# Third-chunk buffers, form loads by ScalarE's queue, sums joined one by one, and a projection moved, in a decoder layer's FFN and embedding stages

## The chip, the cores and the metric

One core of a Trainium2 chip runs the whole kernel in one launch. The metric is the device time in microseconds (us). The kernel before takes 2613.33 us, the median of three runs (2607.94 to 2615.98).

## What is computed

One decoder layer on 512 tokens with 2048 features, all in float32. A mixing part (linear recurrences and RWKV heads) comes first and is not touched here. Then:

```python
u = rmsnorm(h, ln_ffn)                                   # FFN
gate = causal_dwconv(u @ w_gate, conv_f_w, conv_f_b)     # 3 taps; w_gate, w_up: 2048 x 6144
h = h + (gelu(gate) * (u @ w_up)) @ w_down               # w_down: 6144 x 2048

u = rmsnorm(h, ln_ple)                                   # per-layer embedding
e = sigmoid(u @ w_ple_gate) * (p @ w_ple_proj)           # 2048 x 2048 and 256 x 2048
h = h + rmsnorm(e, ln_ple_post)
out = rmsnorm(h, ln_final)
```

## The kernel before

The engines are TensorE (PE; PEld is its weight loads), VectorE (DVE), ScalarE (ACT), GpSimd (POOL) and SyncE (SP). SP issues most transfers, POOL those that add to what is in memory on chip already (L1148, L1178).

**Splits.** Each float32 operand of a matmul is split in two parts of lower precision, `hi` and `lo`, and a product is three matmuls: hi x hi, hi x lo, lo x hi. A weight tile of 512 KB comes by DMA (`wraw`, or a buffer named `x` or `s` where it is combined first), ScalarE makes `whi` (L138) and VectorE `wlo` (L139). `whi` and `wlo` have three buffers each, `wraw` two. Lines 151, 152 and 155 split activations in the same way.

**Products of a block.** A block matrix product is made of seven products of sums of blocks instead of eight. The sums of activations are "forms". The sums of weights come from VectorE (L1131 in the gate stage, L1168 and L1174 in the down stage) and from POOL's adding transfers.

**The gate stage** (about 905 to 1886 us) has 48 units `n`, 24 for each of gate and up side by side. Unit `n` computes seven products, p1, p4, p2, q5, p7, p6, p3, each of 24 matmuls (L1280 to L1282). The order is fixed by hand: behind unit 0's products come the parts of unit 1, 2 and so on, so unit 1's p4 and p6 follow unit 0's p6 closely. p6 and p7 go to the two PSUM banks of the pool `wk`, the others to the six of `mm`. L1306 to L1312 combine the products; L1306 is the first reader of p6. After each even unit `conv` makes the convolution and the GELU (L1325 to L1331), which first multiplies by the tokens' scale of the RMS norm. That scale is spread over the partitions by `rstd_bcast`: four transposing matmuls (L210) into a `wk` bank and a copy by ScalarE (L212). It is called within unit 0, after p6. `spill` writes each finished chunk of the hidden layer to memory as forms (`rd`, `dd`).

**The down stage** (about 1886 to 2334 us) goes through groups of chunks, (0,3), (3,6), (6,9), (9,11), in 14 steps each: two output halves `b` times seven products in the order 1, 0, 4, 2, 3, 5, 6. A step multiplies each of the group's chunks, 12 matmuls a chunk (L1402 to L1404). `load_forms(g, j)` loads the form of product j of group g, three chunks of 256 KB each (L1355); `split_form` splits it two steps later. For the first group the first three forms are loaded during the last unit of the gate stage. Where they sit in SP's queue is up to the scheduler, while the order of VectorE and ScalarE is that of the code (`manual_schedule`, L1438). `down_unit` loads the weights. For product 1 of chunk c it loads two tiles and adds them (L1168); the buffers are given by numbers of `slot`: below 16 they are `x` buffers, from 16 to 43 `s` buffers (number less 16), 44 is the pool `e`. The third chunk's numbers 37, 38 and 39 are s21, s22 and s23, which hold forms of product p2 during the gate stage. After each step the result is copied by ScalarE in the first group (L1430) and added by VectorE in the others (L1428). At the end of each half of the last group seven sums join the seven products (L1435).

**After it** (2334 to 2394) the last chunk and the residual follow for each column block cb = 0, 2, 1, 3: `residual` (loads L1452, transposes L1456, L1458), `down_last` (its end on VectorE is L1468) and `to_features` (transposes L1477, splits L155). **The embedding stage** (2394 to the end) takes each column block's projection, 24 matmuls, and then its gate.

## Time and profile before

| | |
|---|---|
| median of three runs | 2613.33 us (2607.94 to 2615.98) |
| profiled execution | 2613.31 us |
| its span, first to last instruction | 2611.5 us |
| mean TensorE clock granted | 0.988 |
| busy: PE, DVE, ACT, POOL | 2543.5, 1904.5, 1249.5, 228.2 us |
| longest idle times of PE in the stages of the diff | 5.15 us at L210, 3.92 and 3.51 us at L1402, 1.96 us at L1477 and at L1402 |

A row of the waits names the instruction that waited, its releaser, the total in us, how often, and the longest. A row of a timeline has the start, the duration, the engine, line and operation, and in brackets the idle time before it and what ended it. A row of the windows has the busy time of each engine in a stretch with the clock granted to TensorE (1.00 is full speed). What lies between two matmuls' starts, not a matmul's own duration, is its cost in a dense run.

### The profile page before, as it was taken

Reading aid. Unit: us, or ns where it says so; the run is one execution under the profiler, and the core shown is the slowest. Engines: PE = TensorE matmul, PEld = TensorE weight load, DVE = VectorE, ACT = ScalarE, POOL = GpSimd, SP = SyncE. Lnnn points to the kernel's source line nnn. Section 1 sums busy time; section 2 is a strip of 40 time slices with the busy share of each in tenths; the row PEclk is TensorE's granted clock in tenths of the full one; section 3 lists DMA queues with packets and bytes.
Section 4 is the critical chain, followed back from the end, with each engine's and each line's share of the span. In section 5 each row is a group of like instructions: output and inputs, shape, how many; then the busy total and the mean of one; then the engine's idle time right before and its main releaser. Section 6 shows DMA issues by size and latency. Waiting matters only on the chain.

```text
span 2611.5 us, 51670 instructions
## 1 busy us (share of the span) xinstructions
PE 2543.5 (97%) x21922; PEld 2243.9 (86%) x21922; DVE 1904.5 (73%) x2603; ACT 1249.5 (48%) x1735; POOL 228.2 (9%) x251
## 2 busy tenths in 40 slices
PE   9989999999999989999999999999999999999997
PEld 8867777777777889999999999999978877777887
DVE  5764775667575978878788878887777786886447
ACT  6563555547433634444444444444466453434335
POOL 0010100101121010000000000000000000000001
PEclk9999999999999999999999999999999999999999
DMA  7222222222342666776677767777768777743333
GB/s 253 93 70 66 86 78 67 82 82 78 95 141 91 210 166 180 192 184 167 191 188 186 184 170 189 191 178 192 223 171 252 197 218 189 216 109 110 97 95 108
DMA packets 131304, 393.76 MB, mean 151 GB/s; under 512 B 14464, under 2 KB 26624, under 8 KB 131072
## 3 DMA queue, kind: packets, MB, share of 16 engines
q1 hardware_dynamic: 111200, 318.10, 35.9%
q0 software_dynamic: 19872, 72.36, 16.8%
q8 instruction: 171, 2.80, 0.4%
q14 instruction: 61, 0.50, 0.1%
HBM read 353.97 MB, written 36.44 MB: 149 GB/s over the span
## 4 chain that ended last, share of the span: by engine, by line
PE 62%; DVE 5%; DMA 2%; ACT 2%; issue 1%; POOL 0%; ACTq 0%; POOLq 0%; DVEq 0%
PE mm L1282 9%; PE mm L1281 9%; PE mm L1280 9%; PE mm L1403 5%; PE mm L1404 5%; PE mm L1402 5%; PE wk L1281 3%; PE wk L1282 3%; PE wk L1280 3%; PE mm L1519 2%; PE mm L1521 2%; PE mm L1520 2%; PE mm L168 2%; PE mm L170 2%; PE mm L172 1%; DMA wraw<-wd 1%
## 5 line engine op out<-in xcount | busy, mean ns | idle before, releaser
L138 ACT ACTIVATE whi<-x 128x1024 fp32r<-128x1024 f32 x296 | 313.5, 1060 | 441.5 <-PE mm L1281 232.6
L139 DVE TENSOR_TENSOR wlo<-x,whi 128x1024 fp32r<-128x1024 f32 x296 | 361.7, 1223 | 122.6 <-ACT whi L138 116.3
L138 ACT ACTIVATE whi<-wraw 128x1024 fp32r<-128x1024 f32 (+1 forms) x229 | 233.1, 1018 | 382.6 <-PE mm L170 186.4
L1282 PE MATMUL mm<-s,wlo 128*128 128x256 f32 x1432 | 406.3, 284 | 0.7 <-DVE wlo L139 0.7
L1280 PE MATMUL mm<-s,whi 128*128 128x256 f32 x1432 | 406.1, 284 | 0.9 <-ACT s L151 0.9
L139 DVE TENSOR_TENSOR wlo<-wraw,whi 128x1024 fp32r<-128x1024 f32 (+1 forms) x229 | 278.2, 1215 | 176.5 <-ACT whi L138 174.9
L1281 PE MATMUL mm<-s,whi 128*128 128x256 f32 x1432 | 406.1, 284 | 0.2 <-DVE s L152 0.2
L168 PE MATMUL mm<-x,whi 128*128 128x512 f32 x832 | 332.9, 400 | 1.2 <-DVE hT L458 0.9
L172 PE MATMUL mm<-x,wlo 128*128 128x512 f32 x832 | 332.8, 400 | 0.0
L170 PE MATMUL mm<-x,whi 128*128 128x512 f32 x832 | 331.6, 399 | 0.0
L1402 PE MATMUL mm<-whi,s 128*128 128x512 f32 x680 | 268.8, 396 | 10.7 <-ACT whi L138 10.6
L1280 PEld LDWEIGHTS mm<-s,whi 128*128 128x128 f32 x1432 | 275.8, 193 | 1.2 <-ACT s L151 1.1
L1282 PEld LDWEIGHTS mm<-s,wlo 128*128 128x128 f32 x1432 | 275.9, 193 | 0.9 <-DVE wlo L139 0.9
L1281 PEld LDWEIGHTS mm<-s,whi 128*128 128x128 f32 x1432 | 275.7, 193 | 0.4 <-DVE s L152 0.4
L1403 PE MATMUL mm<-wlo,s 128*128 128x512 f32 x680 | 269.9, 397 | 4.0 <-DVE wlo L139 4.0
L1404 PE MATMUL mm<-whi,s 128*128 128x512 f32 x680 | 268.6, 395 | 0.0
L168 PEld LDWEIGHTS mm<-x,whi 128*128 128x128 f32 x832 | 157.5, 189 | 37.2 <-issue 3.0
L172 PEld LDWEIGHTS mm<-x,wlo 128*128 128x128 f32 x832 | 157.5, 189 | 34.0 <-issue 1.9
L170 PEld LDWEIGHTS mm<-x,whi 128*128 128x128 f32 x832 | 157.4, 189 | 33.6 <-issue 1.8
L1148 POOL DMA_DIRECT2D x<-wgu x94 | 82.8, 880 | 955.2 <-DVE wlo L139 654.9
L1280 PE MATMUL wk<-s,whi 128*128 128x256 f32 x584 | 165.3, 283 | 0.0
L1281 PE MATMUL wk<-s,whi 128*128 128x256 f32 x584 | 165.3, 283 | 0.0
(570 smaller groups left out, 5510.6 us busy)
## 6 DMA issues: line engine op xcount, KB each, us to landing
x<-wgu SPq DMA_DIRECT2D x144, 512.0 KB, 4.1
x<-wgu POOLq DMA_DIRECT2D x94, 512.0 KB, 5.5
wraw<-wz SPq DMA_DIRECT2D x80, 512.0 KB, 3.5
wraw<-wgu SPq DMA_DIRECT2D x51, 512.0 KB, 4.1
x<-wd SPq DMA_DIRECT2D x34, 512.0 KB, 5.3
x<-wd POOLq DMA_DIRECT2D x32, 512.0 KB, 5.6
wraw<-wpg SPq DMA_DIRECT2D x31, 512.0 KB, 3.5
wraw<-wd SPq DMA_DIRECT2D x30, 512.0 KB, 4.0
```

What stands on the lines that cost most here:

```text
L138: nc.scalar.activation(hi, raw, AF.Copy)
L139: nc.vector.tensor_tensor(lo, raw, hi.bitcast(F32), ALU.subtract)
L168: nc.tensor.matmul(ps, hi[:, k, :], xh, start=first and i == 0, stop=False)
L170: nc.tensor.matmul(ps, hi[:, k, :], xl, start=False, stop=False)
L172: nc.tensor.matmul(ps, lo[:, k, :], xh, start=False, stop=last and i == n - 1)
L1148: nc.gpsimd.dma_start(g["s"], src(0, 0 if u == "p6" else 1), accum_op=ALU.add)
L1280: TE.matmul(ps, wh[:, k, :], xh, start=k == 0, stop=False)
L1281: TE.matmul(ps, wh[:, k, :], xl, start=False, stop=False)
L1282: TE.matmul(ps, wl[:, k, :], xh, start=False, stop=k == 7)
L1402: TE.matmul(ps, x[0][:, k, ts_], w[0][:, k, :], start=first and k == 0, stop=False)
L1403: TE.matmul(ps, x[0][:, k, ts_], w[1][:, k, :], start=False, stop=False)
L1404: TE.matmul(ps, x[1][:, k, ts_], w[0][:, k, :], start=False, stop=last and k == 1)
```

## The change

Six edits, all behind the mixing part.

1. The third chunk's buffers in the down stage (`down_unit`): s21, s22 and s23 become x13, x14 and x8. The result tiles `PT` that had x8, x13 and x14 move to s23, s21 and s22 in return.
2. `rstd_bcast` and the convolution of unit 0 move from the end of (0, p6) and (0, p3) to the end of (1, p6).
3. `load_form` issues on ScalarE's queue. Only the three forms loaded in the gate stage stay on SP's.
4. The seven sums of the last group's first half are made one after each step of its second half. Those of the second half are placed in the loop over cb: four ahead of `down_last(0)`, three ahead of `down_last(2)`.
5. The projection becomes a function. The one of column block 0 runs between `down_last(3)` and `to_features(3)`, with the loads and splits of the embeddings (`pT`) ahead of it.
6. Buffers of the features (`US`), of the residual and of the gains are numbered through `slot` and partly exchanged.

```diff
         def plain(kh, nh):
             self.pn += 1
-            return load(self.slot((2, 6, 39, 44, 44)[(self.pn - 1) % 5]), kh, nh)
+            return load(self.slot((2, 6, 8, 44, 44)[(self.pn - 1) % 5]), kh, nh)
         if i == 1:
-            self.d0[c], self.d1[c], self.dq[c] = plain(0, 0), load(self.slot((1, 5, 38)[c]), 0, 1), self.slot((0, 3, 37)[c])
+            self.d0[c], self.d1[c], self.dq[c] = plain(0, 0), load(self.slot((1, 5, 14)[c]), 0, 1), self.slot((0, 3, 13)[c])
...
-            if n == 0 and u == "p6":
-                self.rstd_bcast(acc, D, RMS_EPS, k2, rs, rt)
             if n == NF - 1:
                 if u in ("q5", "p1", "p4"):
-                    load_forms(0, ("q5", "p1", "p4").index(u))
+                    load_forms(0, ("q5", "p1", "p4").index(u), nc.sync)
...
-        def load_form(src, tag):
+        def load_form(src, tag, q=nc.scalar):
             t = T("s%d" % tag, 1, (128, 2, 2, 256), F32R)
-            nc.sync.dma_start(t[:, 1].bitcast(F32), src)
+            q.dma_start(t[:, 1].bitcast(F32), src)
...
             unit(n, u)
+            if n == 1 and u == "p6":
+                self.rstd_bcast(acc, D, RMS_EPS, k2, rs, rt)
+                c = B(9)
+                conv(0, o, c)
             if u != "p3":
                 continue
             p, o = n // 2, G_.pop(n)["out"]
+            if n == 0:
+                continue
...
-        PT = {i: [self.slot(n) for n in t] for i, t in enumerate(((43, 40), (8, 41), (15, 42), (4, 13), (12, 11), (7, 14), (10, 9)))}
+        PT = {i: [self.slot(n) for n in t] for i, t in enumerate(((43, 40), (39, 41), (15, 42), (4, 37), (12, 11), (7, 38), (10, 9)))}
...
+                if g + 1 == len(GROUPS) and b == 1:
+                    join(0, j)
...
-            if g + 1 == len(GROUPS):
-                for o, x, y, op in ((2, 2, 0, ALU.add), (5, 5, 0, ALU.add), (6, 6, 4, ALU.add), (6, 6, 2, ALU.add),
-                                    (1, 1, 2, ALU.subtract), (3, 3, 1, ALU.add), (4, 1, 4, ALU.subtract)):
-                    V.tensor_tensor(PT[o][b], PT[x][b], PT[y][b], op)
+        JOIN = ((2, 2, 0, ALU.add), (5, 5, 0, ALU.add), (6, 6, 4, ALU.add), (6, 6, 2, ALU.add),
+                (1, 1, 2, ALU.subtract), (3, 3, 1, ALU.add), (4, 1, 4, ALU.subtract))
+
+        def join(b, j):
+            o, x, y, op = JOIN[j]
+            V.tensor_tensor(PT[o][b], PT[x][b], PT[y][b], op)
...
         for cb in (0, 2, 1, 3):
             residual(cb)
+            if cb % 2 == 0:
+                for j in range(4 if cb == 0 else 3):
+                    join(1, j + 2 * cb)
             down_last(cb)
+            if cb == 3:
+                for k in range(2):
+                    r = T("e", 2, (128, 2, S))[:, 0]
+                    nc.sync.dma_start(r, A["pT"][k])
+                    t_ = self.slot(2 + k, F32R)
+                    self.split(t_[:, 0], t_[:, 1], r)
+                    px.append((t_[:, 0], t_[:, 1]))
+                pp = project()
             to_features(cb)
...
         for cb in range(4):
+            if cb:
+                pp = project()
```

The first place is TensorE in units 0 and 1 of the gate stage: `mm_11083` before and `mm_11077` after is the bank of (1, p4), `wk_11169` that of (1, p6), `wk_11221` that of (1, p7). Before:

```order
4018 L1282 MATMUL mm_10906<-s_1470_10136,wlo_11017 128x256
4019 L1280 MATMUL mm_11083<-s_1451_10117,whi_11045 128x256
4020 L1281 MATMUL mm_11083<-s_1451_10117,whi_11045 128x256
4021 L210 MATMUL wk_11077<-con,rsr_11012 128x128 x4
4022 L1282 MATMUL mm_11083<-s_1451_10117,wlo_11046 128x256
4023 L1280 MATMUL mm_11083<-s_1451_10117,whi_11045 128x256
```

In the new order the same four matmuls of L210 come after all 24 of (1, p6):

```order
4042 L1282 MATMUL mm_11077<-s_1454_10120,wlo_11046 128x256
4043 L1280 MATMUL wk_11169<-s_1455_10121,whi_11079 128x256
...
4066 L1282 MATMUL wk_11169<-s_1458_10124,wlo_11080 128x256
4067 L210 MATMUL wk_11206<-con,rsr_11012 128x128 x4
4068 L1280 MATMUL wk_11221<-s_1459_10125,x_1608_11110 128x256
```

L210 has moved past the rest of (1, p4) and past (1, p6), and the first to ask for the `wk` bank that L1306 frees is now (1, p6).

The second place is SP around the start of the down stage: `s22` and `s23` (before), `x8` (after) take the third chunk's weights, `s0` to `s20` forms, `e` and `x2` later weights. Before:

```order
511 L1355 DMA s12_2921_22050<-dd0_1_10814 128x512
512 L1355 DMA s13_2922_22052<-dd1_1_10816 128x512
513 L1355 DMA s14_2923_22054<-dd2_1_10818 128x512
514 L1355 DMA s15_2932_22116<-rd0_1_10790 128x2x256
515 L1355 DMA s16_2933_22118<-rd1_1_10792 128x2x256
516 L1160 DMA s22_2881_21866<-wd 128x1024
517 L1160 DMA s23_2880_21864<-wd 128x1024
518 L1355 DMA s17_2934_22120<-rd2_1_10794 128x2x256
519 L1160 DMA e_2913_21987<-wd 128x1024
```

And after (L1353 is the same load, L1335 the store to `rd`):

```order
506 L1160 DMA e_2905_21956<-wd 128x1024
507 L125 DMA wraw_2949_22190<-wd 128x1024
508 L1353 DMA s8_2864_21752<-dd2_1_10818 128x512
509 L1160 DMA x8_2880_21864<-wd 128x1024
510 L1160 DMA e_2913_21987<-wd 128x1024
511 L1335 DMA rd11_1_10812<-x11_2843_21606 128x1024
512 L1160 DMA x2_2916_22008<-wd 128x1024
```

The load into x8 follows the ninth form directly, the other of the pair (into x14) stands 22 rows before it, and the forms s9 to s20 are gone from SP. On ScalarE, in the first group, they stand behind the copies of a step; a name in brackets is a semaphore, DMAHW one of the eight that loads use in turn:

```order
1195 L1430 ACTIVATE s_2885_21902<-mm_21985 128x512
1196 L1430 ACTIVATE s_2885_21902<-mm_21986 128x512
1197 L1353 DMA s_2921_22050<-dd_1_10814 128x512 [waits DMAHW7_49]
1198 L1353 DMA s_2922_22052<-dd_1_10816 128x512 [waits DMAHW1_49]
1199 L1353 DMA s_2923_22054<-dd_1_10818 128x512 [waits DMAHW2_49]
1200 L138 ACTIVATE whi_22059<-x_2871_21797 128x1024 [waits DMASW6_49,PE_49,Activation_49]
```

Each of the three waits until an earlier load that used the same semaphore has landed, and the split L138 stands behind them.

The third place is VectorE at the turn from the first to the second half of the last group. L1435 (before) and L1444 (after) are the joins, L1428 and L1432 the sums of a step. Before:

```order
2262 L1428 TENSOR_TENSOR x_2897_21914<-x_2897_21914,mm_24873 128x512
2263 L1435 TENSOR_TENSOR x_2889_21906<-x_2889_21906,s_2885_21902 128x1024
2264 L1435 TENSOR_TENSOR x_2895_21912<-x_2895_21912,s_2885_21902 128x1024
2265 L1435 TENSOR_TENSOR x_2897_21914<-x_2897_21914,x_2893_21910 128x1024
2266 L1435 TENSOR_TENSOR x_2897_21914<-x_2897_21914,x_2889_21906 128x1024
2267 L1435 TENSOR_TENSOR x_2887_21904<-x_2887_21904,x_2889_21906 128x1024
2268 L1458 SCALAR_TENSOR_TENSOR x_2895_21912<-x_2895_21912,rsr_11012,wk_25202 128x512
2269 L1435 TENSOR_TENSOR x_2891_21908<-x_2891_21908,x_2887_21904 128x1024
2270 L1435 TENSOR_TENSOR x_2893_21910<-x_2887_21904,x_2893_21910 128x1024
2271 L1174 TENSOR_TENSOR x_3431_24826<-x_3431_24826,s_3448_24917 128x1024
```

After:

```order
2269 L1432 TENSOR_TENSOR s_2888_21905<-s_2888_21905,mm_24909 128x512
2270 L1444 TENSOR_TENSOR x_2889_21906<-x_2889_21906,s_2885_21902 128x1024
2271 L139 TENSOR_TENSOR wlo_24955<-x_3436_24848,whi_24954 128x1024
2272 L139 TENSOR_TENSOR wlo_24972<-x_3432_24828,whi_24971 128x1024
2273 L1432 TENSOR_TENSOR s_2886_21903<-s_2886_21903,mm_24951 128x512
2274 L1432 TENSOR_TENSOR s_2886_21903<-s_2886_21903,mm_24952 128x512
2275 L1444 TENSOR_TENSOR x_2895_21912<-x_2895_21912,s_2885_21902 128x1024
```

One join now follows the sums of each step, with the weights' splits (L139) of the next step between two joins; L1458, the residual's sum, stands behind the stage.

More of the change, by code (lines that the diff above doesn't have):

```diff
@@ L1364, in load_forms @@
                     src = dd[ch][(i - 1) // 2][:, (i - 1) % 2]
-                hids[ch, i] = load_form(src, 3 * j + ch - lo)
+                hids[ch, i] = load_form(src, 3 * j + ch - lo, q)
         def split_form(g, j, ch):
@@ L1446, in phase2 @@
         ss3 = k2.tile([128, 16], F32, name="ss3")
-        US = (0, 1, 3, 4, 6, 7, 9, 10, 12, 13, 15, 16, 18, 19, 21, 22)
+        US = (16, 17, 19, 20, 22, 23, 25, 26, 28, 29, 31, 32, 34, 35, 13, 14)
         def residual(cb):
-            hr = [T("s%d" % n, 1, (128, 2, S)) for n in {0: (14, 17), 2: (20, 21), 1: (14, 17), 3: (20, 22)}[cb]]
+            hr = [self.slot(n) for n in {0: (30, 33), 2: (36, 13), 1: (30, 33), 3: (36, 14)}[cb]]
             for i in range(2):
@@ L1458, in residual, with project @@
                 V.scalar_tensor_tensor(h, h, rt[:, tt:tt + 1], pt, ALU.mult, ALU.add)
+        def project():
+            ph, pl = self.wnext()
+            p2 = [self.slot(5 + i) for i in range(2)]
+            pp = [p2[tt // 2][:, tt % 2] for tt in range(4)]
+            for tt in range(4):
+                ps = self.mm()
+                ts_ = slice(tt * 128, (tt + 1) * 128)
+                for k in range(2):
+                    TE.matmul(ps, px[k][0][:, ts_], ph[:, k, :], start=k == 0, stop=False)
+                    TE.matmul(ps, px[k][0][:, ts_], pl[:, k, :], start=False, stop=False)
+                    TE.matmul(ps, px[k][1][:, ts_], ph[:, k, :], start=False, stop=k == 1)
+                SC.activation(pp[tt], ps, AF.Copy)
+            return pp
         def down_last(cb):
@@ L1493, in phase2 @@
             nc.sync.dma_start(gfin[i], A["gains"][1:2, i * S:(i + 1) * S].broadcast_to([128, S]))
-        px = []
-        for k in range(2):
-            r = T("e", 2, (128, 2, S))[:, 0]
-            nc.sync.dma_start(r, A["pT"][k])
-            t_ = self.slot(2 + k, F32R)
-            self.split(t_[:, 0], t_[:, 1], r)
-            px.append((t_[:, 0], t_[:, 1]))
         rsh = k2.tile([128, 4], F32, name="rsh")
@@ L1507, in phase2 @@
         MU, AD = ALU.mult, ALU.add
-        et = [self.slot(n) for n in (8, 15, 40, 41, 42, 43, 0, 1)]
+        et = [self.slot(n) for n in (39, 15, 40, 41, 42, 43, 0, 1)]
         e = [et[i % 8][:, i // 8] for i in range(16)]
@@ L1589, in phase2 @@
         for cb in range(4):
-            ph, pl = self.wnext()
-            p2 = [self.slot(5 + i) for i in range(2)]
-            pp = [p2[tt // 2][:, tt % 2] for tt in range(4)]
-            for tt in range(4):
-                ps = self.mm()
-                ts_ = slice(tt * 128, (tt + 1) * 128)
-                for k in range(2):
-                    TE.matmul(ps, px[k][0][:, ts_], ph[:, k, :], start=k == 0, stop=False)
-                    TE.matmul(ps, px[k][0][:, ts_], pl[:, k, :], start=False, stop=False)
-                    TE.matmul(ps, px[k][1][:, ts_], ph[:, k, :], start=False, stop=k == 1)
-                SC.activation(pp[tt], ps, AF.Copy)
+            if cb:
+                pp = project()
             if cb == 0:
```

8 lines of the change are left out of this document (5 added, 3 removed).

## The prediction

> **What bounds the kernel now.** I read the page first, then the waits of TensorE (PE), then the windows and the timelines around each wait.
>
> ```profile
> span 2611.5 us, 51670 instructions
> PE 2543.5 (97%) x21922; PEld 2243.9 (86%) x21922; DVE 1904.5 (73%) x2603; ACT 1249.5 (48%) x1735; POOL 228.2 (9%) x251
> PE mm L1402 <- ACT whi L138: 10.6, 5, 3.9
> PE wk L210 <- DVE e L1306: 5.2, 1, 5.2
> PE mm L1403 <- DVE wlo L139: 4.0, 6, 0.8
> PE wk L1477 <- DVE s L155: 2.0, 1, 2.0
> ```
>
> TensorE is busy for 97% of the span, and the change takes no matmul away. What can be won is idle time of PE, 2611.5 - 2543.5 = 68 us in all, plus what its clock loses behind an idle stretch. The wait rows (who waited for whom, total us, times, longest) name four kinds that lie in the stages the diff touches, 21.8 us together. The price of each place is its idle time, plus the busy time of each window behind it multiplied by one minus the clock granted there. The windows' rows: length, then busy time of PE, PEld, DVE, ACT, POOL, then the clock PEclk, the DMA share, GB/s.
>
> ```profile
> 940.00:945.00 5.00, 4.05 (x19) 4.08 (x20) 4.86 (x8) 0.60 (x1) 0.00 (x0) 0.50 1.02 223
> 945.00:950.00 5.00, 5.00 (x37) 5.00 (x37) 1.87 (x3) 2.47 (x3) 0.00 (x0) 0.83 0.29 92
> 1895.00:1900.00 5.00, 4.06 (x9) 3.00 (x10) 4.85 (x6) 3.05 (x5) 0.86 (x1) 0.56 1.03 283
> 1900.00:1905.00 5.00, 5.00 (x18) 4.03 (x17) 3.37 (x4) 2.70 (x5) 0.00 (x0) 0.75 0.94 220
> 2175.00:2180.00 5.00, 4.24 (x13) 3.35 (x13) 5.00 (x6) 1.42 (x2) 0.00 (x0) 0.66 0.35 105
> 2235.00:2240.00 5.00, 3.87 (x10) 2.86 (x11) 4.64 (x6) 3.26 (x5) 0.00 (x0) 0.70 0.52 166
> 2300.00:2305.00 5.00, 3.01 (x7) 2.43 (x8) 5.00 (x6) 2.12 (x2) 0.00 (x0) 0.68 0.00 0
> 2390.00:2395.00 5.00, 2.85 (x15) 1.66 (x13) 3.59 (x9) 5.00 (x11) 1.03 (x1) 0.90 0.69 208
> 2395.00:2400.00 5.00, 4.86 (x17) 3.81 (x17) 2.23 (x4) 1.35 (x3) 0.00 (x0) 0.76 0.01 2
> ```
>
> **Part A, the broadcast of the FFN's scale (L210).**
>
> ```profile
> 935.40 0.28 PE L1280 MATMUL mm<-s,whi 128*128 128x256 f32 x1
> 935.52 0.28 PE L1281 MATMUL mm<-s,whi 128*128 128x256 f32 x1
> 940.95 2.05 PE L210 MATMUL wk<-con,rsr 128*128 128x128 f32 x8 [5.15 <-DVE e L1306]
> 935.88 1.06 ACT L138 ACTIVATE whi<-x 128x1024 fp32r<-128x1024 f32 x1 [3.59 <-DMA x<-wgu]
> 940.38 0.42 DVE L1306 TENSOR_TENSOR e<-wk,e 128x256 f32<-128x256 f32 x1
> PE mm L1402 <- ACT whi L138: 2.0, 1, 2.0
> ```
>
> L210 stands two matmuls into the product (1, p4) and needs a PSUM bank that L1306 frees at 940.80. L1306 is late because VectorE, in order, first has to split weights whose load only let ScalarE begin at 935.88. The loss is 5.15 + 4.05 x 0.50 + 5.00 x 0.17 = 8.0 us. L1306 keeps its place among VectorE's instructions, so the bank is free at the same time. After the change the other 22 matmuls of (1, p4) run first, each 0.12 us after the one before (935.40, 935.52), until 938.3; then (1, p6) waits for that same bank. So 2.7 us of idle time stay, and the clock behind them. For the clock I take the nearest rows: a wait of 2.0 us, the third chunk's at 2174.6 (last row), and 5.00 - 4.24 = 0.76 us more were followed by a clock of 0.66, a loss of 4.24 x 0.34 = 1.4 us. So A keeps 4.1 and gains **3.9 us**; if the clock still loses as much as now (2.9), the gain is 2.4. The Trainium skill, "TensorE: Matmul & The Clock Gate", section "Why this matters for your kernels", asks for no idle gaps over about 3 us, since one idle window brings half clock; by that rule 2.7 us cost no clock and A gains 5.3. The row of 0.66 behind shorter gaps speaks against it.
>
> **Part F, 72 form loads from SP's queue to ScalarE's.** SP issues 81 of them before (L1355); 9 stay there.
>
> ```profile
> 2220.93 1.06 ACT L138 ACTIVATE whi<-x 128x1024 fp32r<-128x1024 f32 x1 [1.14 <-PE mm L1404]
> 2223.65 1.06 ACT L138 ACTIVATE whi<-wraw 128x1024 fp32r<-128x1024 f32 x1 [1.66 <-PE mm L1404]
> 2234.27 1.06 ACT L138 ACTIVATE whi<-wraw 128x1024 fp32r<-128x1024 f32 x1 [6.32 <-DMA wraw<-wd]
> DMA to landing us min/median/max: 3.5/7.2/9.2
> 1865.84 0.38 SPq L1355 DMA_DIRECT2D s<-dd  x1
> 1876.15 4.16 SPq L1355 DMA_DIRECT2D s<-dd  x7
> ```
>
> The trace has no DMA issued by ScalarE. The nearest rows are SP's: 0.38 us alone, 4.16 / 7 = 0.59 in a row. Three in a step are 1.1 to 1.8 us of ScalarE. It idles 1.14 us in a chunk in which it also splits a form, 3.4 us in a step of three chunks, so the issue is hidden: 0. Two late loads of wraw (the landing row is of nine of them) make PE wait near 2174 and 2235; the second costs 5.00 - 3.87 + 3.87 x 0.30 = 2.3 us. The first has no form load beside it in the order of before, and the forms beside the second share the DMA engines with it whoever issues them. I count 0 for both.
>
> **Part B, the third chunk's weights at the start of the down stage.**
>
> ```profile
> 1881.01 0.74 DVE L1330 SCALAR_TENSOR_TENSOR x<-x,par,x 128x511 f32<-128x511 f32 x1
> 1882.63 1.06 SPq L1160 DMA_DIRECT2D s<-wd  x2
> 1892.74 1.22 DVE L1168 TENSOR_TENSOR s<-s,s 128x1024 f32<-128x1024 f32 x1 [4.49 <-DMA s<-wd]
> 1895.15 1.23 DVE L139 TENSOR_TENSOR wlo<-s,whi 128x1024 fp32r<-128x1024 f32 x1 [1.18 <-ACT whi L138]
> 1895.17 0.49 PE L1402 MATMUL mm<-whi,s 128*128 128x512 f32 x1 [3.51 <-ACT whi L138]
> 1896.43 0.80 PE L1403 MATMUL mm<-wlo,s 128*128 128x512 f32 x1 [0.77 <-DVE wlo L139]
> x<-wd SPq DMA_DIRECT2D x34, 512.0 KB, 5.3
> ```
>
> Both loads go into buffers that the last unit's X forms hold, so SP issues them at 1882.63, behind the row of form loads of part F, and VectorE can add them ten us later. Loss: 3.51 + 0.77 + 4.06 x 0.44 + 5.00 x 0.25 = 7.3 us. After the change the one into x14 stands many loads earlier on SP, and the one into x8 waits only for the last reader of x8, the convolution that ends at 1881.01 + 0.74 = 1881.75; twelve form loads have left that queue. With the median landing of 5.3 us the data are there at 1887.1, L1168 ends at 1888.3, L138 at 1889.4, L139 at 1890.6. PE wants the chunk at 1895.17 - 3.51 = 1891.7, so 1.1 us are to spare. I leave 1.0 us for what comes late next, the splits of the following step: **6.3 us**. If the load takes the 9.2 us of the slowest wraw, the same chain ends at 1894.5: 2.5 idle and 1.4 of clock stay, and B gains 3.4.
>
> **Part G, the sums of the last group.**
>
> ```profile
> 2290.82 2.35 DVE L1435 TENSOR_TENSOR x<-x,s 128x1024 f32<-128x1024 f32 x2
> 2293.09 3.62 DVE L1435 TENSOR_TENSOR x<-x,x 128x1024 f32<-128x1024 f32 x3
> 2297.28 2.35 DVE L1435 TENSOR_TENSOR x<-x,x 128x1024 f32<-128x1024 f32 x2
> 2301.99 0.79 PE L1402 MATMUL mm<-whi,s 128*128 128x512 f32 x1 [3.92 <-ACT whi L138]
> PE wk L1456 <- DVE x L1458: 0.6, 1, 0.6
> 2308.87 1.28 DVE L1428 TENSOR_TENSOR s<-s,mm 128x512 f32<-128x512 f32 x2
> ```
>
> Seven joins in a row, 8.3 us, hold back the next weights' splits. Loss: 3.92 + 0.6 + 3.01 x 0.32 = 5.5 us. After the change one join follows each step of two chunks, 2 x 2.72 = 5.44 us of PE (ScalarE's splits of part F start 2.72 us apart). VectorE then has 2 x 1.23 + 1.28 + 1.2 = 4.9 us in a step, and PE hides it. In two steps the new order has a second join, 6.1 against 5.44; with 0.5 us left for these, G gains **5.0**. If both show in full and the clock falls as now, it is 3.1. The transposes of residual(0), which now lie in this place, move behind the stage and are done once either way.
>
> **Part H, the projection.** The wait of 2.0 us at L1477 lies in the windows from 2390 on: 2.15 idle, 2.85 x 0.10 and 4.86 x 0.24 of clock, 3.6 us. PE waits there until VectorE, busy with the end of down_last(3), reaches L155. After the change 24 matmuls of the projection stand ahead of those transposes, 24 x 2.72 / 12 = 5.4 us (a chunk has 12 of the same size), more than the wait. They need weights of their own and four PSUM banks, two of which VectorE still has to free: I take **2.5 us**, between 0 and 3.6.
>
> **Sum.** 3.9 + 6.3 + 5.0 + 2.5 = 17.7. The profiled execution took 2613.31 us, 1.8 more than its span, and the median of the runs is 2613.33, so the sum needs no correction: 2613.3 - 17.7 = **2595.6 us**.
>
> **Rivals.** (1) The late wraw at 2234 goes too, since SP's queue is freer: 2593.3. For it, form loads stand between the weights there; against it, the wait at 2174 has none and is as long: 0.14. The Trainium skill, "DMA: Bandwidth & Descriptors", section "Issuing engines are not separate DMA queues", says that issuing from more engines saves issue time alone; by that rule the wait stays. (2) What is left of A's gap loses no clock, 1.4 less, 2594.2; the clock of 0.66 behind shorter gaps speaks against it: 0.08. It is the page's rule of part A. (3) B does not do what it says: x8 or its load is as late as the old buffers were, 6.3 less gain, 2601.9. The chain has 1.1 us to spare: 0.12. (4) ScalarE's queue becomes the bound. In the new order a form load waits until an earlier load, in a rotation of eight, has landed, and behind it on ScalarE stand L138 and the evacuations of PSUM (L1430), for which PE waits. The earlier load was let go at least a step before, 3 x 2.72 = 8.2 us, against landings of 7.2 (median) to 9.2; ScalarE has 3.4 - 1.8 = 1.6 us a step to spare. Forms are loaded in 25 steps. At 0.5 us a step lost by PE 12.5 come back and the time is 2608.1, no change; at 1.2 us it is 2625.6, slower. Slower begins at (17.7 + 7.8) / 25 = 1.0 us a step, landings of 8.2 + 1.6 + 1.0 = 10.8 us on average, above any row. 0.11 for the first size, 0.06 for the second.
>
> **How the numbers follow.** 0.3%, 7.8 us, is about what a measurement of this kernel can tell from no change. The forecast has 0.49, the rivals 0.14, 0.08, 0.12, 0.11 and 0.06. All but the two sizes of (4) are faster: 0.83, 0.11, 0.06. The low end takes every upper bound, 5.3 + 7.3 + 5.5 + 3.6 + 2.3 = 24.0: 2589. The high end takes 2.4 + 3.4 + 3.1 + 0 = 8.9 and gives back 3.6 us by rival (4), 0.14 a step: 2608.
>
> **What would show it.** L210 waits no longer and (1, p6) waits 2.7 us for L1306; no wait of L1402 near 1892 or 2302; none of L1477 near 2392; the two behind wraw stay. The forecast is wrong if the matmuls of the down stage wait for L138 or L139 step after step, and its cause is rival (4) if ScalarE's own rows there show idle time that a DMA ends.

## The result and the profile after

The kernel after takes **2589.4 us** (median of 6 runs, 2585.56 to 2594.65) against 2610.91 us of the kernel before (6 runs, 2607.94 to 2615.98): a ratio of 0.9916, with a 95% interval of 0.9899 to 0.9932. It is faster by 21.5 us, where 17.7 were forecast. The profiled execution of after took 2585.56 us and is the fastest of its six.

First the head of its page, and then the waits of TensorE (who waited for whom: us, times, longest) in the down stage, from 1878 to 2375 us.

```profile
span 2583.8 us, 51614 instructions
PE 2530.0 (98%) x21922; PEld 2235.2 (87%) x21922; DVE 1902.9 (74%) x2603; ACT 1249.4 (48%) x1735; POOL 227.8 (9%) x251
```

```profile
PE mm L1407 <- DVE wlo L139: 3.5, 6, 0.8
PE mm L1406 <- ACT whi L138: 2.2, 4, 1.0
PE mm L1406 <- ACT s L151: 0.6, 1, 0.6
```

TensorE has the same 21922 matmuls and is busy for 98%. Lines 1406 to 1408 are before's 1402 to 1404. The waits for L138 have shrunk from 10.6 us with a longest of 3.9 to 2.2 us with a longest of 1.0; those for L139 have gone from 4.0 to 3.5 us, six times in both, with a longest of 0.8. L1500 (before's L1477) and L1466 (before's L1456) are in no wait row of this stage.

The timeline of after at the start of the down stage and at the gate stage's unit 1 (start us, duration, engine, line; in brackets what it waited for):

```profile
1876.90 0.33 SPq L1160 DMA_DIRECT2D x<-wd  x1
1881.21 1.23 DVE L1168 TENSOR_TENSOR x<-x,x 128x1024 f32<-128x1024 f32 x1 [1.40 <-DMA x<-wd]
1882.53 2.01 ACT L138 ACTIVATE whi<-x 128x1024 fp32r<-128x1024 f32 x2 [4.54 <-DVE x L1168]
939.73 0.36 PE L1280 MATMUL wk<-s,whi 128*128 128x256 f32 x1 [1.22 <-DVE e L1306]
```

The third chunk's weights are added at 1881.2, 0.8 us behind the stage's first matmul (1880.4), and split at 1882.5; before, the sum came 6.7 us behind it (1892.7 against 1886.0). No matmul of the stage's start waits. In the gate stage it is now a product matmul, L1280, that waits for the bank of L1306, as the prediction had it. It waits 1.2 us here, and in a second profiled execution of the same kernel 2.8.

**Where the time went.** The kernel's stages follow one another on TensorE, so the first and last start of a line mark them off. The gate stage is counted from the first L1280 to the first matmul of the down stage, that one to its last matmul, then the way to the first matmul of the embedding gate (L1519, now L1547), that gate, and the tail. Two such rows, of before and of after, with first and last start in us:

```profile
L1402 PE MATMUL mm<-whi,s x680: 387/389/792, 1886.0 to 2388.6; 128*128 128x512 f32 x170
```

```profile
L1406 PE MATMUL mm<-whi,s x680: 387/389/505, 1880.4 to 2366.2; 128*128 128x512 f32 x170
```

Each kernel was profiled twice (the second time as runs before_again and after_again, below):

| us | before | again | after | again | gain, mean |
|---|---|---|---|---|---|
| ahead of the gate stage | 905.1 | 908.9 | 902.2 | 902.8 | 4.5 |
| gate stage | 980.9 | 982.6 | 978.2 | 978.5 | 3.4 |
| down stage | 502.6 | 501.5 | 485.8 | 486.1 | 16.1 |
| to the embedding gate | 12.6 | 11.6 | 6.9 | 6.9 | 5.2 |
| embedding gate | 194.0 | 193.9 | 195.1 | 195.1 | -1.2 |
| tail | 16.3 | 16.4 | 15.6 | 15.6 | 0.8 |

The first row is code that the change doesn't touch. It lies between 900.0 and 909.0 us in all thirteen profiled executions of this study, so a single execution's total says little to 9 us. The rows behind it repeat within 2 us. They add up to 24.3 us, the medians of the runs to 21.5. The two profiled executions of after are the fastest of their six and of their five, and the second of before is the slowest of its twelve, so the 24.3 us lean to the high side.

### The profile page after: what moved, and what is told of

It is laid out like the page before. It is cut to its first block, busy times and chain, and to the rows that moved or that the text cites. A ratio compares the mean times of both kernels' runs of the same rounds, so it can differ in the third digit from the quotient of the medians.

```text
span 2583.8 us, 51614 instructions
## 1 busy us (share of the span) xinstructions
PE 2530.0 (98%) x21922; PEld 2235.2 (87%) x21922; DVE 1902.9 (74%) x2603; ACT 1249.4 (48%) x1735; POOL 227.8 (9%) x251
## 4 chain that ended last, share of the span: by engine, by line
PE 63%; DVE 4%; DMA 2%; ACT 1%; issue 1%; POOL 0%; POOLq 0%; ACTq 0%; DVEq 0%
PE mm L1282 9%; PE mm L1281 9%; PE mm L1280 9%; PE mm L1407 5%; PE mm L1408 5%; PE mm L1406 5%; PE wk L1280 3%; PE wk L1282 3%; PE wk L1281 3%; PE mm L1547 2%; PE mm L1549 2%; PE mm L1548 2%; PE mm L168 2%; PE mm L170 2%; PE mm L172 2%; DMA wraw<-wd 1%
## 5 line engine op out<-in xcount | busy, mean ns | idle before, releaser
L138 ACT ACTIVATE whi<-x 128x1024 fp32r<-128x1024 f32 x329 | 348.5, 1060 | 482.3 <-PE mm L1281 230.7
L139 DVE TENSOR_TENSOR wlo<-x,whi 128x1024 fp32r<-128x1024 f32 x329 | 402.3, 1224 | 137.5 <-ACT whi L138 131.2
L138 ACT ACTIVATE whi<-wraw 128x1024 fp32r<-128x1024 f32 (+1 forms) x229 | 233.1, 1018 | 382.7 <-PE mm L170 182.4
L1280 PE MATMUL mm<-s,whi 128*128 128x256 f32 x1432 | 406.1, 284 | 2.1 <-ACT whi L138 1.4
L139 DVE TENSOR_TENSOR wlo<-wraw,whi 128x1024 fp32r<-128x1024 f32 (+1 forms) x229 | 278.2, 1215 | 170.6 <-ACT whi L138 169.1
L1280 PEld LDWEIGHTS mm<-s,whi 128*128 128x128 f32 x1432 | 275.6, 192 | 2.5 <-ACT whi L138 1.6
L1406 PE MATMUL mm<-whi,s 128*128 128x512 f32 x680 | 265.2, 392 | 2.8 <-ACT whi L138 2.2
L1408 PE MATMUL mm<-whi,s 128*128 128x512 f32 x680 | 265.7, 391 | 0.1
L1280 PE MATMUL wk<-s,whi 128*128 128x256 f32 x584 | 165.4, 283 | 1.2 <-DVE e L1306 1.2
L1282 PE MATMUL wk<-s,wlo 128*128 128x256 f32 x584 | 165.3, 283 | 0.0
```

What stands on the lines that cost most here:

```text
L138: nc.scalar.activation(hi, raw, AF.Copy)
L139: nc.vector.tensor_tensor(lo, raw, hi.bitcast(F32), ALU.subtract)
L1280: TE.matmul(ps, wh[:, k, :], xh, start=k == 0, stop=False)
L1282: TE.matmul(ps, wl[:, k, :], xh, start=False, stop=k == 7)
L1406: TE.matmul(ps, x[0][:, k, ts_], w[0][:, k, :], start=first and k == 0, stop=False)
L1408: TE.matmul(ps, x[1][:, k, ts_], w[0][:, k, :], start=False, stop=last and k == 1)
```

## The experiments

Two theories stood at first. By the first, each part of the change wins in its own place what the prediction gave it, and the sum is only too small. By the second, the order of loads on the two queues does most of it, and buffers and joins are worth little. Unless said otherwise, each kernel is after with one edit.

To compare them I count matmuls. Undisturbed, TensorE starts 442 to 444 matmuls of the down stage in 100 us, one in 0.225 us, and 112 in 25 us (rows of third_raw, below). Six places of the stage lose most of what is lost in the first 400 us. (A seventh, near +235, costs 0.6 us in every kernel with two `wraw`, and project_late loses 1.3 us more near +164.) In a window of 25 us at each, what is missing to 112 times 0.225 us is the loss, the idle time and the clock together, good to a matmul or two. The first two of these windows in before (length; busy time and count of PE, PEld, DVE, ACT, POOL; clock; DMA share; GB/s) and then the same places in after:

```profile
1886.00:1911.00 25.00, 20.73 (x79) 16.33 (x78) 16.64 (x17) 10.41 (x14) 1.73 (x2) 0.86 0.92 278
1916.00:1941.00 25.00, 25.00 (x112) 20.72 (x111) 15.14 (x17) 16.74 (x25) 2.39 (x3) 1.00 0.69 174
...
2156.00:2181.00 25.00, 22.28 (x91) 17.79 (x90) 12.21 (x13) 8.09 (x8) 1.75 (x2) 0.93 0.62 169
2221.00:2246.00 25.00, 23.36 (x95) 18.62 (x94) 16.85 (x21) 10.79 (x13) 0.89 (x1) 0.93 0.85 276
```

```profile
1880.40:1905.40 25.00, 25.00 (x113) 20.69 (x112) 20.55 (x22) 15.74 (x22) 2.54 (x3) 1.00 0.94 291
1910.40:1935.40 25.00, 24.01 (x104) 19.11 (x103) 15.51 (x18) 16.39 (x23) 1.76 (x2) 1.00 0.73 219
...
2150.40:2175.40 25.00, 23.73 (x104) 19.11 (x103) 16.92 (x18) 8.44 (x9) 1.76 (x2) 1.00 0.50 143
2215.40:2240.40 25.00, 24.08 (x106) 19.37 (x105) 19.65 (x24) 12.00 (x15) 0.87 (x1) 1.00 0.74 228
```

At the start before loses 112 - 79 = 33 matmuls, 7.4 us, and after none; 30 us on it is before that loses none and after 8, 1.8 us. All kernels, matmuls missing at each place (us behind the stage's first matmul), with the length of the down stage:

| kernel | +0 | +30 | +90 | +210 | +270 | +335 | stage, us |
|---|---|---|---|---|---|---|---|
| before | 33 | 0 | 8 | 8 | 21 | 17 | 502.6 |
| before_again | 33 | 0 | 6 | 8 | 21 | 8 | 501.5 |
| after | 0 | 8 | 9 | 11 | 8 | 6 | 485.8 |
| after_again | 0 | 6 | 6 | 11 | 19 | 5 | 486.1 |
| old_bufs | 17 | 12 | 8 | 8 | 8 | 9 | 490.4 |
| forms_sp | 13 | 3 | 10 | 9 | 18 | 9 | 490.2 |
| old_bufs_sp | 27 | 0 | 14 | 6 | 10 | 7 | 491.5 |
| act_only | 19 | 13 | 7 | 9 | 9 | 7 | 497.2 |
| joins_burst | 0 | 3 | 7 | 11 | 9 | 4 | 492.0 |
| project_late | 0 | 2 | 6 | 10 | 18 | 18 | 489.9 |
| bcast_early | 0 | 20 | 7 | 8 | 12 | 8 | 488.2 |
| third_raw | 0 | 0 | 0 | 0 | 0 | 0 | 475.4 |
| third_raw_sp | 1 | 0 | 0 | 0 | 0 | 0 | 475.6 |

### old_bufs: the third chunk in its old buffers

```diff
-            return load(self.slot((2, 6, 8, 44, 44)[(self.pn - 1) % 5]), kh, nh)
+            return load(self.slot((2, 6, 39, 44, 44)[(self.pn - 1) % 5]), kh, nh)
...
-            self.d0[c], self.d1[c], self.dq[c] = plain(0, 0), load(self.slot((1, 5, 14)[c]), 0, 1), self.slot((0, 3, 13)[c])
+            self.d0[c], self.d1[c], self.dq[c] = plain(0, 0), load(self.slot((1, 5, 38)[c]), 0, 1), self.slot((0, 3, 37)[c])
```

The later users of these buffers change with it.

> The changed kernel with the third chunk's weights back in s21 to s23 (and the result tiles back in x8, x13, x14); form loads stay on ScalarE's queue. Theory: the buffers set the wait, so PE waits again about 3.5 + 0.8 us near 1887 with a clock below 1 behind it: 6.5 us more than the changed kernel's 2589.4, 2596. Rival: the form loads in front of and beside the two loads set it. With twelve of them gone the two loads land about 5 us after 1877, the third chunk is ready in time, PE waits under 1 us there, and the time is 2589 to 2591.

Measured: 2592.02 us (2590.53 to 2595.31), ratio 0.9931 [0.9916, 0.9947]. Its waits of TensorE:

```profile
PE mm L1406 <- ACT whi L138: 4.6, 5, 2.5
```

The wait at the start comes back with 2.5 us (and 0.8 for L139), not with before's 3.5, and 17 matmuls are lost, 3.8 us, not 33. So the buffers alone are about half of part B in this execution. The time, 2592.0, lies between the 2596 of the theory and the 2591 of the rival.

### forms_sp: the forms back on SP's queue

```diff
-        def load_form(src, tag, q=nc.scalar):
+        def load_form(src, tag, q=nc.sync):
...
-        def load_forms(g, j, q=nc.scalar):
+        def load_forms(g, j, q=nc.sync):
```

> The changed kernel with all form loads on SP's queue again. Theory: which queue issues a form does not matter to the late loads of wraw, because the DMA engines are shared; PE's two waits behind wraw (near 2163 and 2224) stay at 1.0 to 1.5 us each with no fall of the clock, and the time is within 2 us of 2589.4, apart from what the start of the down stage loses if the load into x8 falls behind forms. Rival: SP's queue between the weights made wraw late, so these two waits grow to 2.7 and 1.7 us with a clock of about 0.7 behind them: 4.9 us more, 2594.3 or above.

Measured: 2590.53 us (2585.93 to 2597.14), ratio 0.9930 [0.9913, 0.9947].

```profile
PE mm L1406 <- ACT whi L138: 4.8, 5, 1.7
PE mm L1407 <- DVE wlo L139: 4.2, 7, 0.8
```

With the new buffers and the old queue the start waits again, 1.7 + 0.8 us, 13 matmuls. The queue that I had counted at 0 carries the other half of B in this execution. The load into x8 is issued 3.5 us ahead of the stage's first matmul, as in after, but the sum of the weights starts 8.4 us behind the issue instead of 4.3, with six forms issued on the same queue just ahead of it. That these forms slow the load is argued, not shown: third_raw_sp (below) has them on SP's queue as well and loses one matmul at the start. The two waits behind wraw are 1.8 us, with a fall of the clock, and 1.5, so neither the theory nor the rival was met there. ScalarE's queue isn't what bounds the kernel either, since without it the time is the same within the interval.

### old_bufs_sp: both undone

It has the edits of old_bufs and forms_sp together.

> The changed kernel with the third chunk's old buffers and all form loads on SP: part B undone as a whole. Theory: buffers and queue act only together. Each undone alone gave waits of 3.3 and 2.5 us without a fall of the clock; both undone give the kernel before's 3.5 + 0.8 us and a clock near 0.5 behind it, 7.3 us above the changed kernel, 2597. Rival: the two waits simply add, 5.8 us or more of idle time.

Measured: 2596.42 us (2589.16 to 2597.84), ratio 0.9933 [0.9921, 0.9945]. At the start it waits 3.3 + 0.8 us and loses 27 matmuls, near before's 33 and near the 17 + 13 of the two single edits. The theory's time, 2597, was met; the clock fell for half as long as in before.

### joins_burst: the joins of the first half in one go

```diff
-                if g + 1 == len(GROUPS) and b == 1:
-                    join(0, j)
...
+            if g + 1 == len(GROUPS) and b == 0:
+                for j in range(7):
+                    join(0, j)
```

> The changed kernel with the first half's seven sums in one row again at the end of that half. Theory: L1406 waits about 4 us for L138 near 2280 and the clock falls behind it: 5.5 us more, 2595. Rival: what held VectorE back in the kernel before was the residual's sum and transposes among the joins, which now stand behind the stage; then the buffers of three splits cover the 8.3 us, the wait is under 1.5 us, and the time is 2590 to 2591.

Measured: 2598.16 us (2590.38 to 2602.09), ratio 0.9951 [0.9934, 0.9969]. Its waits and the windows behind the joins:

```profile
PE mm L1406 <- ACT whi L138: 5.5, 4, 3.9
...
PE wk L1466 <- DVE x L1468: 0.6, 1, 0.6
```

```profile
2278.00:2283.00 5.00, 0.66 (x4) 0.42 (x4) 5.00 (x6) 1.06 (x1) 0.00 (x0) 0.91 0.00 0
2283.00:2288.00 5.00, 5.00 (x12) 3.93 (x13) 5.00 (x6) 1.06 (x1) 0.00 (x0) 0.50 0.00 0
2288.00:2293.00 5.00, 5.00 (x22) 4.05 (x21) 4.07 (x6) 2.12 (x2) 0.87 (x1) 0.91 0.15 14
```

The same 3.9 and 0.6 us come back, so the rival falls. The clock behind them is at 0.50 for 6.8 us, where it was for 3.4 us in the profile of before that I priced. The stage is 16.6 us longer than third_raw's; 34 missing matmuls are 7.7 of it, so 8.9 us lie here. By the same count it is 27.2 - 87 x 0.225 = 7.6 us in before, 9.0 in before_again, and 1.0 and 0.1 in the two profiles of after. These remainders also hold what the six windows miss. The records of all kernels have the same 2040 matmuls in this stage; comparing matmul by matmul with third_raw, the joins and what follows cost 6.9 us in before, 7.8 in before_again, 8.3 in joins_burst and nothing in either profile of after.

### project_late: the projection behind the last transposes

```diff
             down_last(cb)
+            to_features(cb)
             if cb == 3:
...
                 pp = project()
-            to_features(cb)
```

> The changed kernel with the first projection and the embeddings' splits behind to_features(3) again. Theory: the profiles' marks say that this edit is worth 5.3 us (12.6 us between the last matmul of down_last and the first of the gate before, 6.9 after, with 24 matmuls in both): 2594.7, with a wait of 2 us for L155. Rival: it is worth what the wait and the clock of the busy rows say, 3.6 us at most, and half of it is lost elsewhere: 2591 to 2593.

Measured: 2593.64 us (2589.22 to 2597.51), ratio 0.9937 [0.9921, 0.9954].

```profile
PE wk L1500 <- DVE s L155: 2.0, 1, 2.0
...
PE mm L1479 <- DVE x L152: 0.7, 1, 0.7
```

The 2.0 us behind the down stage are back, and the projection itself then waits for 0.7 us. From the last matmul of the down stage to the tail it takes 11.7 + 194.0 = 205.7 us, as before (206.6 and 205.5); after takes 6.9 + 195.1 = 202.0. Part H is worth 3.5 to 4.6 us. The median of the runs, 2593.64, lies between the theory's and the rival's.

### after_again and before_again: no edit

> The changed kernel once more, unedited. Theory: behind waits of 1 to 2 us the clock falls in some executions and not in others, and the part before the FFN, the same in both kernels, varies by several us between executions. Then this profile shows the same waits behind wraw (within 0.5 us each) with or without a fall of the clock, the down stage takes 486 to 491 us, and the median is 2588 to 2593. Rival: the changed kernel never loses clock there, the down stage takes 485 to 487 us again, and what remains of difference lies ahead of the FFN.

> The kernel before once more, unedited. Theory: the waits near 2174 and 2235 return within 0.5 us (2.8 and 1.7), since they belong to the loads, while the falls of the clock behind them may be missing; the down stage takes 498 to 503 us. Rival: these two waits are chance themselves, shrink to the 1.3 and 1.0 us of the changed kernel, and the 4.9 us between the kernels there are no effect of the change.

Measured: after_again 2590.26 us (5 runs), ratio 0.9910 [0.9895, 0.9925]; before_again 2613.69 us (12 runs), ratio 1.0001 [0.9992, 1.0010]. The result repeats. Of the waits behind wraw, near 285 and 345 us of the stage, before_again has 2.6 and 1.4 us against 2.7 and 1.6, as expected. after_again has 2.0 and 0.8 against 1.3 and 0.9, the first more than 0.5 us off, and a fall of the clock behind it that after did not have. So these waits vary from execution to execution, but in before they are not chance alone. In after_again the place in the gate stage is as forecast, both in the wait and in the clock of the second window:

```profile
PE wk L1280 <- DVE e L1306: 2.8, 1, 2.8
```

```profile
935.00:940.00 5.00, 2.23 (x20) 2.05 (x18) 4.00 (x5) 3.77 (x4) 0.87 (x1) 0.99 0.29 64
940.00:945.00 5.00, 5.00 (x30) 5.00 (x31) 4.46 (x7) 0.54 (x1) 0.54 (x1) 0.67 0.92 254
```

### bcast_early: the scale's broadcast back in its place

```diff
+            if n == 0 and u == "p6":
+                self.rstd_bcast(acc, D, RMS_EPS, k2, rs, rt)
...
-            if n == 1 and u == "p6":
-                self.rstd_bcast(acc, D, RMS_EPS, k2, rs, rt)
-                c = B(9)
-                conv(0, o, c)
...
-            if n == 0:
-                continue
```

> The changed kernel with the broadcast and the first convolution back in unit 0. Theory: L210 waits 5 us again and the gate stage takes about 981 us instead of 978.2: 2.7 us more, 2592. Rival: the clock fell between 930 and 935 in the changed kernel for another reason (a late load of the unit before), which this kernel does not have, so that the edit is worth under 1 us and the time is 2589 to 2590.

Measured: 2596.02 us (2591.13 to 2596.92), ratio 0.9931 [0.9916, 0.9947].

```profile
PE wk L210 <- DVE e L1306: 3.1, 1, 3.1
```

The convolution behind it goes back with it. L210 waits again, and the gate stage takes 982.2 us as with the old place elsewhere (980.9, 982.6, and 982.5 in act_only), against 977.3 to 979.8 in the nine with the new place. Part A is worth about 3.3 us. The rival falls: the clock is lowered between 930 and 935 in this kernel too (0.74, behind a wait of 1.9 us for L138). The median is 5.8 us above that of after_again, more than this stage shows; the profile also loses 20 matmuls at +30.

### act_only: before with the forms on ScalarE's queue

The edit of forms_sp the other way, in before, without the first three steps' forms.

> The kernel before with nothing but the form loads moved to ScalarE's queue (the three forms loaded in the gate stage stay on SP's). Theory: the third chunk's wait shrinks from 4.3 to about 3.3 us, because twelve forms no longer load beside it, and the rest stays: 1 to 3 us less than the kernel before (2610.9), the waits behind wraw as there. Rival: the queue makes most of the gain, both waits behind wraw shrink to about 1 us and the time is 6 us or more below the kernel before.

Measured: 2607.58 us (11 runs), ratio 0.9982 [0.9972, 0.9993].

```profile
PE mm L1402 <- ACT whi L138: 6.6, 5, 3.9
...
PE mm L1402 <- ACT s L151: 1.6, 1, 1.6
```

The queue alone brings the start down from 33 to 19 missing matmuls, 3.2 us, and loses 13, 2.9 us, 30 us later, where a form's split (L151) now is late: it stands on ScalarE behind the split of a `wraw` that starts only 8.5 us after its load was issued. The waits behind wraw near +285 and +345 are 1.3 and 0.9 us, as the rival had it, but the time is only 4.3 us below that of before in the same set of runs (2611.91), more than the theory's 3 and less than the rival's 6. With the joins' and the projection's shares above, the second of the two theories falls: buffers and joins are worth more than the queue.

### third_raw and third_raw_sp: a buffer of its own for the third chunk's fifth tile

In after the places from +30 on have one thing in common. The split that is late reads a `wraw`, and the waits come at product 5, whose three tiles share the two `wraw`. One of them in after:

```profile
2152.68 1.23 DVE L139 TENSOR_TENSOR wlo<-wraw,whi 128x1024 fp32r<-128x1024 f32 x1 [0.30 <-ACT whi L138]
2153.93 10.56 SPq L125 DMA_DIRECT2D wraw<-wd  x3
2161.82 1.06 ACT L138 ACTIVATE whi<-wraw 128x1024 fp32r<-128x1024 f32 x1 [6.45 <-DMA wraw<-wd]
2162.04 0.39 PE L1408 MATMUL mm<-whi,s 128*128 128x512 f32 x1
2162.93 0.49 PE L1406 MATMUL mm<-whi,s 128*128 128x512 f32 x1 [0.50 <-ACT whi L138]
2164.18 0.50 PE L1407 MATMUL mm<-wlo,s 128*128 128x512 f32 x1 [0.77 <-DVE wlo L139]
2164.52 0.39 PE L1408 MATMUL mm<-whi,s 128*128 128x512 f32 x1
```

The split L139 of the first chunk's tile ends at 2153.91, SP issues the third load at 2153.93, and its split starts 7.9 us later. The new theory: the third load can start only when the first chunk's tile has been split, and it is this that is left, whoever issues the forms. Then a buffer of its own, x14, which is idle at that point of a group, takes all the waits away. By the rival, the waits come from the DMA engines' share that the forms take, and stay. third_raw_sp has the forms on SP's queue besides.

```diff
+        if i == 5:
+            return load(self.slot(14), 1, 0)
...
-                        if i == 5:
+                        if i == 5 and ch - lo < 2:
```

> The changed kernel with the third chunk's tile of product 5 loaded into x14, which is free two steps earlier, instead of into one of the two wraw buffers. Theory: the waits that are left in the down stage (0.2 to 1.4 us for L138 or L151 and 0.8 for L139, at 45, 105, 225, 285 and 345 us of the stage) come from that load alone, which is let go only when the first chunk's tile has been split. They go, with the falls of the clock behind them: 4 to 8 us less, 2582 to 2586, and the down stage takes under 484 us. Rival: those loads are late because the DMA engines are full there, and an earlier load only makes another late: under 2 us.

> The same edit, and all form loads on SP's queue. Theory: with wraw out of the way, the queue of the forms matters only at the start of the down stage, where the load into x8 stands behind forms on SP (2.5 us as in the run with the forms on SP): 2 to 4 us above the kernel with the edit alone. Rival: the forms on ScalarE cost more than they bring (ScalarE waits for the rotation of loads), so this one is as fast or faster.

Measured: third_raw 2579.78 us (4 runs, 2579.46 to 2580.37), ratio 0.9875 [0.9862, 0.9887]; third_raw_sp 2577.06 us (4 runs, 2572.76 to 2583.97), ratio 0.9873 [0.9857, 0.9888]. Both beat both kernels. Windows of third_raw:

```profile
1885.00:1985.00 100.00, 100.00 (x444) 82.82 (x443) 71.05 (x72) 62.26 (x84) 9.67 (x11) 1.00 0.86 247
...
2085.00:2185.00 100.00, 100.00 (x442) 82.79 (x442) 83.50 (x94) 49.50 (x58) 9.37 (x11) 1.00 0.73 198
2185.00:2285.00 100.00, 100.00 (x443) 82.79 (x442) 85.27 (x97) 48.23 (x55) 8.79 (x10) 1.00 0.75 209
```

TensorE waits for nothing in the down stage any more, at full clock, and the stage takes 475.4 us (475.6 with the forms on SP). The rival falls: the forms are loaded as in after, and the earlier load makes no other late. The gain is larger than the 4 to 8 us expected. For third_raw_sp it is the rival's time that was met: it is as fast, and the wait expected at the start of the stage isn't there. What was left in after is 485.8 - 475.4 = 10.4 us, though its waits add up to 6.3 us and its clock was not lowered there. The rows above show the rest: the matmuls start 0.89, 1.25 and 0.34 us apart where 0.23 would be undisturbed, 1.8 us lost in all, and the two waits named are 0.50 + 0.77 = 1.27. An idle time is counted from a matmul's end, 0.39 us behind its start, while undisturbed the next one would have started after 0.23.

## Why the prediction was right in kind and too small

The forecast, 2595.6 us, had the direction and the mechanisms of A, B, G and H right. The time, 2589.4, is at the low end of the range, 2589, which was worked out as the sum of all upper bounds. So the bounds failed too: G's lay below all that was measured, and the bound for the late `wraw` held one wait of two. What failed are the price of the joins (G) and of the projection (H), and the 0 for the late `wraw` (F). By the mean of two profiles each, behind the untouched part ahead:

| step | forecast | measured |
|---|---|---|
| A, broadcast | 3.9 | 3.4 |
| B, start of the down stage | 6.3 | 7.4, less 1.6 at +30 |
| F, the late `wraw` (+90 to +335) | 0 | 2.5 |
| G, joins | 5.0 | 7.8 (7.4 matmul by matmul) |
| H, projection | 2.5 | 4.0 |
| tail | none | 0.8 |
| sum | 17.7 | 24.3 |

**A** came as worked out in kind: L210 waits no longer, and L1280 waits 1.2 or 2.8 us for the same bank. That the size fits too is in part luck. In after_again the clock falls to 0.67 behind the 2.8 us, where 0.66 had been taken from a row. In after it does not fall behind the 1.2 us (1.00 from 940 to 945) but ahead of them, to 0.73 from 930 to 935, behind a wait of 1.4 us for L138 that the priced profile of before did not have. The Trainium skill's rule ("TensorE: Matmul & The Clock Gate", section "Why this matters for your kernels"), that there be no idle gaps over about 3 us, would have given 5.3 if shorter ones cost no clock. Rival (2), which was made of it, holds at this place in after and not in after_again, whose 2.8 us cost 5.00 x 0.33 = 1.7 us more.

**B** did what it says, against rival (3): the whole 7.4 us at the start are won. The chain held: L138 of the third chunk ends 3.2 us behind the stage's first matmul (1883.6), where 1889.4 - 1886.0 = 3.4 was worked out. (For the slow load the chain's own ends give 1894.5 - 1891.7 = 2.8 us of idle time, not 2.5.) The reason given was half of it. That the twelve forms leave SP's queue was in the chain, but F was booked at 0 as if it were a part on its own, and old_bufs and forms_sp show that buffers and queue carry about half each, though third_raw_sp starts without a wait with the forms on SP's queue. The remainder of 1.0 us that I left "for what comes late next" is 1.6, and its place is +30, the first product 5.

**F: the 0 for the late `wraw` failed**, though not as rival (1) had it. The waits stayed, in after and in every kernel with two `wraw`: near +285 and +345 (in the windows at +270 and +335) they are 2.7 and 1.6 us in before, 2.6 and 1.4 in before_again, 1.3 and 0.9 in after, 2.0 and 0.8 in after_again. With their length varies the clock behind them. At +270 a kernel loses 18 to 21 matmuls where the mean clock of the 25 us is 0.93 (before, before_again, after_again, forms_sp, project_late) and 8 to 12 where it is 1.00 (the other six): about 2.2 us, from whether the clock falls and from the longer waits that go with it. At +335 it is 17 and 18 against 4 to 9. Before happened to have the fall at both places, after at none. Whether the change makes the fall rarer isn't settled: with the forms on SP it came in three of four kernels at +270, on ScalarE in two of seven. The rule of the Trainium skill named at rival (1), "DMA: Bandwidth & Descriptors", section "Issuing engines are not separate DMA queues", agrees with third_raw and third_raw_sp: with the buffer shortage gone, the queue makes 475.4 against 475.6 us.

**G and H: the size of the loss failed**, "3.92 + 0.6 + 3.01 x 0.32 = 5.5" and "2.15 idle, 2.85 x 0.10 and 4.86 x 0.24 of clock, 3.6". G loses 6.9 to 8.3 us, matmul by matmul, and H 3.5 to 4.6. For G three reasons are shown. The first is a wrong reading: the mean clock of a window, 0.68, was multiplied with the work of a window that was partly idle. All of that work ran at half clock; the full clock lay over the idle time. Before:

```profile
2302.58 0.63 PE L1403 MATMUL mm<-wlo,s 128*128 128x512 f32 x1
2303.01 0.63 PE L1404 MATMUL mm<-whi,s 128*128 128x512 f32 x1
```

```profile
2301.84:2305.25 3.41, 3.26 (x8) 2.58 (x9) 3.41 (x5) 1.16 (x2) 0.00 (x0) 0.50 0.00 0
```

The starts lie 0.43 us apart instead of 0.23, so 3.01 x 0.50 = 1.5 us are lost there, not 1.0. The second reason is that the price was read from one execution: the clock was low for 3.4 us in before, for 6.8 in before_again and joins_burst. The third is that idle time and clock together leave out what the matmuls around a wait lose; at 2162 us in after that was 1.8 us for 1.27. So G's upper bound lay below everything measured. For H the price of 3.6 was near, and what I held back of it for weights and PSUM banks was not needed: no wait is left behind the down stage in after. The cover that I doubted, VectorE's second join in two steps, held: no wait is left in that place.

**Rival (4)** did not come: no matmul waits step after step. Of the kernels with two `wraw`, those with forms on ScalarE's queue lose 2 to 20 matmuls at +30, those with forms on SP 0 to 3. But ScalarE waits there for a load of `wraw` (5.55 us in after), not for the rotation of form loads, and third_raw, with its forms on ScalarE's queue, loses none. From its issue to its split this load takes 8.6 us in bcast_early, which loses 20 matmuls, and 6.2 in project_late, which loses 2; why it differs is not settled.

## What to carry to other kernels

Price a wait of TensorE by counting: the matmuls started in a window around it, against a window of the same code without a wait, and multiply what is missing by the undisturbed spacing; that takes in the idle time, the clock and the slow starts at once. Read it from two executions, since the clock's part is there in one and missing in the other, and let the upper bound hold the fall. The mean clock of a window says nothing of its work where part of the window is idle. And when a stall goes, look for the resource that all the waits left have in common: here a pair of buffers for three tiles, which was worth 10.4 us in the stage, more than any single part of the change.

## What the runs showed of the hardware

The length of a wait didn't decide alone whether the clock fell; where it lay did too. Between 900 and 2395 us of all thirteen traces the granted clock is 1.00 or 0.50, and a fall lasts 3.41 us or twice that. Within one execution all falls begin at whole multiples of 3.41 us from one another. (A window of 5.00 us that holds one of 3.41 shows 1 - 0.5 x 3.41 / 5.00 = 0.66.) Divided along these multiples, this stretch of the thirteen traces has 5641 windows of 3.41 us at full clock, and 33 of them are followed by a fall. TensorE is busy in these for at most 52%, and only four others are as little busy (45 to 49%). So a window about half idle was followed by a fall, and a wait that two windows share could pass without one.

In old_bufs TensorE stood still for 2.5 and 0.8 us around a few matmuls; two windows share the 3.3 us, and there was no fall:

```profile
1889.44:1892.85 3.41, 1.54 (x7) 0.94 (x5) 1.23 (x1) 0.47 (x1) 0.87 (x1) 1.00 0.79 310
1892.85:1896.26 3.41, 2.01 (x8) 1.44 (x9) 2.79 (x3) 3.41 (x5) 0.00 (x0) 1.00 0.96 150
1896.26:1899.68 3.42, 3.42 (x17) 2.83 (x16) 3.42 (x5) 2.22 (x5) 0.86 (x1) 1.00 0.69 179
```

In project_late 1.8 us of idle time in one window were enough:

```profile
2226.75:2230.16 3.41, 1.63 (x6) 1.14 (x7) 2.40 (x4) 3.41 (x5) 0.00 (x0) 1.00 0.61 177
2230.16:2233.57 3.41, 3.41 (x10) 2.63 (x9) 3.41 (x5) 0.88 (x3) 0.00 (x0) 0.50 0.42 145
```

A DMA that ScalarE issues takes it 0.33 to 0.53 us for the `dd` forms and 0.53 to 1.25 for the `rd` forms in after (min, median, max in ns):

```profile
L1353 ACTq DMA_DIRECT2D s<-dd x38: 326/443/526, 1888.8 to 2220.8; - x38
```

```profile
L1353 ACTq DMA_DIRECT2D s<-rd x34: 525/622/1252, 1905.1 to 2250.1; - x34
```
